# Gate and up products of a gated block: pairs with features in the partitions, regrouped as quads with tokens in the partitions

## The chip, the cores and the metric

One Trainium2 core (of the eight of a chip) runs one layer of an encoder block on 512 tokens of width 1024. The metric is the device time of one execution in microseconds. Names of engines: TensorE (PE; its weight loads are PEld), VectorE (DVE), ScalarE (ACT), GpSimd (POOL), SyncE (SP). [...]

## The reference, cut to what matters

The change lies in the last third, the feed-forward part and the last norm:

```python
h2 = rmsnorm(x, g_ffn[l])
x = x + (jax.nn.silu(h2 @ w_ff_gate[l]) * (h2 @ w_ff_up[l])) @ w_ff_down[l]
return rmsnorm(x, g_final)
```

`h2` is 512 x 1024, `w_ff_gate` and `w_ff_up` are 1024 x 2816 each, `w_ff_down` is 2816 x 1024, all in float32.

## The kernel before

**Products.** Every float32 product is made of three matmuls on split operands: `hi` is the value rounded to the matmul's type by ACT (a CAST, line 203), `lo` is the rest, which DVE makes by a subtraction (line 204); hi·hi, hi·lo and lo·hi are added up in PSUM. Most matrix products of the kernel are then done by a scheme of Strassen's kind: seven products of half-size blocks in place of eight. Each needs a sum of blocks of the weights (`b11`, `t1` to `t4`, `b21`, `b22`; `t1` = b11+b12, `t2` = t1+b22, `t3` = b12+b22, `t4` = t2+b21 in the kernel's signs) and a sum of blocks of the activations (`a11`, `a12`, `a22`, `s1` to `s4`; `XF` holds those of `h2`).

**The feed-forward part before.** The 2816 columns of gate and up are cut into eleven slices of 256. A **pair** (`pair`, with `first_tokens` for two of its products) computes one slice of both. It is feature-major: a 128 x 128 block of the weights is the stationary operand, and the activations of 256 tokens pass over it (`prod`, line 383: 24 matmuls of 256 columns for each of seven products). So the result has features in the partitions, which is what the down product needs, and `gated` (lines 1138 to 1155) makes `silu(gate) * up` and the seven activation forms of the down product from it, slice by slice. The **down** product (`down`, through `strassen` and `prod_tm`, line 427) is token-major: activations stationary, 512 columns of weights moving. It runs after slices 0 to 2, 3 to 6 and 7 to 10 (`FF_PARTS`). The first part's result goes to a buffer `first_part` in device memory, and eight adding DMAs (`add_first`, line 1208) bring it to the sum `ydr` later, behind a one-element POOL instruction `mark` (line 1247) that holds them until slice 3 is gated. The second part adds itself to `ydr`; the last is added to what is read back of it, then normed and stored.

**Weights.** Raw weight tiles of 128 x 1024 come by SP's queue into ten buffers (`load_raws`, line 286). `prefetch_form` adds two raw tiles on DVE where a sum is wanted (line 301) and splits the sum into one of five hi/lo buffers. A product of a pair uses one such tile; a product of a down part uses up to two. `take` prepares two tiles ahead of the product that runs. For the quads in `SUMMED` (two of the eleven pairs, and the product with `w_o`) the four sums are made earlier by adding DMAs of POOL in device memory (lines 272 and 274), and DVE has only the splits.

**Order.** Each engine runs its own list of instructions in a fixed order, decided when the kernel is built from the order of the code and the buffers; an instruction that waits holds up all behind it on its engine, and a DMA that waits holds up its queue.

Of the kernel before, what the change touches and what calls it, by code (L numbers as in the profile page):

```python
# [41 lines left out]
FF_PARTS = ((0, 3), (3, 4), (7, 4))  # L42
# [11 lines left out]
WIDTH = {"w": 512, "x": 256, "a": 512, "o": 512, "f": 256, "d": 512}  # L54
# [4 lines left out]


FIRST_PRODUCTS = ((0, "b11"), (0, "b21"), (1, "b11"), (1, "b21"), (2, "b11"), (2, "b21"))


def beside(q):

    if q < 5:
        return None, ((q + 6) // 2, "b21" if q % 2 else "b11")
    return (q, "b21"), (q + 1, "b11") if q + 1 < NQ else None


def plan():
# [42 lines left out]
    def f(q, *names):  # L114
        for n in names:
            out.append(("q", ("f", q), n, 0, 4))

    for q, name in FIRST_PRODUCTS:
        f(q, name)
    for q0, n in FF_PARTS:  # L120
        for q in range(q0, q0 + n):
            between, behind = beside(q)
            f(q, "t1", "t2")
            if between:
                f(*between)
            f(q, "t3")
            if behind:
                f(*behind)
            f(q, "t4", "b22")
        units = [(name, u) for name in FORMS for u in range(0, n, 2)]  # L130
        if q0 + n == NQ:

            i = units.index(("b21", 2))
            units[i:i + 3] = units[i + 1:i + 3] + units[i:i + 1]
        for name, u in units:
            out.append(("q", ("d", q0), name, u, min(2, n - u)))
    return out
# [9 lines left out]
SUMMED = (("f", 0), ("f", 1), ("o",))  # L147


def parts(quad):  # L150
    return (0, 2) if quad == ("o",) else (0,)
# [20 lines left out]
def block_kernel(ctx: ExitStack, tc: tile.TileContext, xw0, xw, xT, xtok, wpack, wquad, cols, decs, rot, g_ffn, g_final, out):  # L172
# [25 lines left out]
    low_of = [None]  # L198

    def split(src, hi, lo, scale=None, round=None):  # L200
# [4 lines left out]
        else:  # L205
# [3 lines left out]
                op0=ALU.mult, op1=ALU.subtract)  # L209
        return first  # L210
# [51 lines left out]

    steps = {"quads": sums_of(SUMMED[:2]), "heads": sums_of(SUMMED[2:])}

# [25 lines left out]
    def prefetch_form(quad, f, u, nk):  # L290
# [9 lines left out]
        if more:  # L300
            nc.vector.tensor_tensor(out=t, in0=t, in1=raws[quad, more, u][:, 0:n], op=ALU.add)  # L301
        hi, lo = unit()
        split(t, hi[:, 0:n], lo[:, 0:n])
        return [(hi, lo)]

    def prefetch(first=False, loads=None, splits=None):
# [11 lines left out]
        ready.append((x, units))  # L318
        return True
# [708 lines left out]
    def complete(nb, half, last):  # L1028
        yt, ac = y[half][:, nb, :], acs[nb]
        nc.sync.dma_start(ydr[nb * P:(nb + 1) * P, half * 512:(half + 1) * 512], yt)  # L1030
# [83 lines left out]
    gates = {}  # L1114

    q_add, gate_of = FF_PARTS[1][0], [None]

    def act_tiles(names):
        hi, lo = bigtile(F32R), bigtile(F32R)
        for j, n in enumerate(names):  # L1120
            act[n] = tuple(t[:, 2 * j:2 * j + 2, :].rearrange("p a (b c) -> p (a b) c", c=256) for t in (hi, lo))
        return hi.rearrange("p (f a) (b c) -> p f (a b) c", f=2, c=256), \
            lo.rearrange("p (f a) (b c) -> p f (a b) c", f=2, c=256)

    def gated(q, th, g, u):

        q0, _ = part_of[q]
        i = q - q0  # L1130
        if not gates.get(q0):
            t = bigtile(F32R)
            gates[q0] = [act_tiles(("a11", "a12")), act_tiles(("s1", "s3")), act_tiles(("s2", "s4"))]
            act["a22"] = tuple(t[:, 2 * j:2 * j + 2, :].rearrange("p a (b c) -> p (a b) c", c=256)
                               for j in range(2))
# [3 lines left out]
        nc.vector.tensor_tensor(out=s, in0=u, in1=s, op=ALU.mult)  # L1139

        def both(j, t):
            split(t.rearrange("p (s t) -> p s t", s=2), *(x[:, :, i, :] for x in gates[q0][j]))
        E, O = slice(0, 256), slice(256, 512)
        if th == 1:
            split(s[:, O], *(x[:, i, :] for x in act["a22"]))
        else:
            both(0, s)
        gates[q, th] = s
        if (q, 1 - th) not in gates:
            return  # L1150
# [273 lines left out]
```

## Time and profile before

| what | value |
|---|---|
| three timed runs | 1023.89, 1023.9, 1024.5 us; median 1023.9 |
| span of the profiled execution, first to last instruction | 1021.7 us (the page has no time of its own for it) |
| granted TensorE clock, mean | 0.999 |
| feed-forward part in the trace | from about 683.9 us to the end |
| DMA traffic | 202.34 MB, 198 GB/s mean |

The page's first part says how long each engine was busy; the chain of waits follows the execution back from its last instruction to what released each step. Rows with "xN" merge N instructions. An instruction's time runs from its start to its end, and the next one on the same engine may start before that end, so the distance between starts, not the listed duration, says how many fit into a stretch.

### The profile page before, as it was taken

How to read it: one execution, taken by the hardware profiler on the slowest of the kernel's cores; microseconds unless marked ns; L12 is line 12 of the kernel's file. 1: busy time of each engine (PE TensorE's matmuls, PEld its weight loads, DVE VectorE, ACT ScalarE, POOL GpSimd, SP SyncE). 2: the span in 40 equal slices, each digit the busy share in tenths (PEclk: the TensorE clock that was granted, in tenths of full speed). 3: DMA queues.
4: the chain of work that ended last, by engine and by line, in shares of the span. 5: the costliest groups of instructions: out<-in, count | busy, mean ns of one | idle time of the engine just before them, and what ended most of it. 6: DMA issues, size and time to landing. Idle time of an engine off the chain costs nothing.

```text
span 1021.7 us, 14821 instructions
## 1 busy us (share of the span) xinstructions
PE 1013.2 (99%) x5586; PEld 883.2 (86%) x5586; DVE 902.5 (88%) x1161; ACT 548.4 (54%) x744; POOL 151.7 (15%) x238
## 2 busy tenths in 40 slices
PE   9999999999999999999999999999999999999997
PEld 7888888888888998888888888889998999899986
DVE  7878998979798888797989997999898999889996
ACT  7547665553655455343543325586654565556554
POOL 0030221222122003202122100020001410110011
PEclk9999999999999999999999999999999999999999
DMA  9525587695767657839597855484316562663523
GB/s 354 188 81 185 173 296 212 214 310 162 249 196 238 250 203 268 333 130 349 124 331 294 272 200 169 157 264 132 107 42 242 172 154 83 198 153 104 165 69 98
DMA packets 53992, 202.34 MB, mean 198 GB/s; under 512 B 7392, under 2 KB 7520, under 8 KB 49312
## 3 DMA queue, kind: packets, MB, share of 16 engines
q1 hardware_dynamic: 37600, 137.39, 39.0%
q0 software_dynamic: 16032, 63.71, 21.3%
q8 instruction: 44, 0.72, 0.3%
q10 hardware_dynamic: 288, 0.29, 0.1%
q14 instruction: 28, 0.23, 0.1%
HBM read 162.82 MB, written 57.41 MB: 216 GB/s over the span
## 4 chain that ended last, share of the span: by engine, by line
PE 98%; DVE 1%; ACT 0%; issue 0%; POOL 0%; POOLq 0%; ACTq 0%
PE bank L427 39%; PE bank L383 27%; PE bank L342 10%; PE bank L343 10%; PE bank L344 10%; PE bank L477 0%; PE bank L1053 0%; PE bank L998 0%; PE bank L662 0%; DVE raw L301 0%; DVE big L1296 0%; ACT whi L203 0%; DVE wlo L204 0%; POOL fin L1286 0%; POOL ac L1035 0%
## 5 line engine op out<-in xcount | busy, mean ns | idle before, releaser
L203 ACT CAST whi<-raw 128x1024 fp32r<-128x1024 f32 (+2 forms) x299 | 302.8, 1028 | 265.0 <-PE bank L427 67.1
L204 DVE TENSOR_TENSOR wlo<-raw,whi 128x1024 fp32r<-128x1024 f32 (+2 forms) x300 | 352.7, 1192 | 68.0 <-ACT whi L203 67.7
L383 PE MATMUL bank<-xform,whi 128*128 128x256 f32 x1424 | 258.2, 284 | 0.3 <-ACT whi L203 0.3
L383 PEld LDWEIGHTS bank<-xform,whi 128*128 128x128 f32 x1424 | 222.3, 192 | 2.0 <-ACT t L434 0.8
L383 PE MATMUL bank<-xform,wlo 128*128 128x256 f32 x712 | 200.7, 283 | 0.0
L427 PE MATMUL bank<-whi,big 128*128 128x512 f32 x596 | 187.0, 389 | 0.0
L427 PE MATMUL bank<-whi,xform 128*128 128x512 f32 x496 | 157.1, 390 | 0.0
L301 DVE TENSOR_TENSOR raw<-raw 128x1024 f32<-128x1024 f32 (+1 forms) x128 | 152.0, 1203 | 4.2 <-DMA raw<-wquad 3.3
L383 PEld LDWEIGHTS bank<-xform,wlo 128*128 128x128 f32 x712 | 136.4, 192 | 0.0
L427 PEld LDWEIGHTS bank<-whi,big 128*128 128x128 f32 x596 | 111.9, 188 | 23.8 <-ACT t L434 0.4
L427 PE MATMUL bank<-wlo,big 128*128 128x512 f32 x298 | 115.7, 389 | 0.0
L427 PEld LDWEIGHTS bank<-whi,xform 128*128 128x128 f32 x496 | 93.0, 188 | 19.7 <-DVE xform L204 0.6
L427 PE MATMUL bank<-wlo,xform 128*128 128x512 f32 x248 | 96.5, 389 | 0.0
L434 ACT COPY t<-bank 128x512 f32<-128x512 f32 x105 | 61.0, 587 | 56.3 <-PE bank L383 30.1
L342 PE MATMUL bank<-big,whi 128*128 128x512 f32 x220 | 85.7, 390 | 0.0
L344 PE MATMUL bank<-big,wlo 128*128 128x512 f32 x220 | 85.6, 389 | 0.0
L343 PE MATMUL bank<-big,whi 128*128 128x512 f32 x220 | 85.6, 389 | 0.0
L427 PEld LDWEIGHTS bank<-wlo,big 128*128 128x128 f32 x298 | 56.0, 188 | 11.4
L427 PEld LDWEIGHTS bank<-wlo,xform 128*128 128x128 f32 x248 | 46.6, 188 | 9.6
L342 PE MATMUL bank<-whi,big 128*128 128x512 f32 x128 | 49.8, 389 | 0.0
L343 PE MATMUL bank<-wlo,big 128*128 128x512 f32 x128 | 49.8, 389 | 0.0
L344 PE MATMUL bank<-whi,big 128*128 128x512 f32 x128 | 49.8, 389 | 0.0
(203 smaller groups left out, 1385.8 us busy)
## 6 DMA issues: line engine op xcount, KB each, us to landing
raw<-wquad SPq DMA_DIRECT2D x140, 512.0 KB, 4.7
raw<-wpack SPq DMA_DIRECT2D x42, 512.0 KB, 6.3
t_f<-wquad POOLq DMA_DIRECT2D x12, 512.0 KB, 8.0
z<-t POOLq DMA_DIRECT2D x24, 256.0 KB, 4.5
t_o<-wquad POOLq DMA_DIRECT2D x12, 512.0 KB, 6.7
zform<-z POOLq DMA_DIRECT2D x6, 1024.0 KB, 7.8
v<-t POOLq DMA_DIRECT2D x16, 256.0 KB, 5.7
sg<-t POOLq DMA_DIRECT2D x16, 256.0 KB, 4.8
```

Of the source, the lines that this page charges most:

```text
L203: first = (round or nc.scalar.copy)(hi, src)
L204: low_of[0] = nc.vector.tensor_tensor(out=lo, in0=src, in1=hi.bitcast(F32), op=ALU.subtract)
L301: nc.vector.tensor_tensor(out=t, in0=t, in1=raws[quad, more, u][:, 0:n], op=ALU.add)
L342: nc.tensor.matmul(ps, lh, rh, start=first, stop=False)
L343: nc.tensor.matmul(ps, lh, rl, start=False, stop=False)
L344: nc.tensor.matmul(ps, ll, rh, start=False, stop=last)
L383: nc.tensor.matmul(o, l[:, c], r[:, k], start=start and s == 0 and k == 0 and i == 0, stop=stop and k == 3 and i == 2, skip_group_check=True)
L427: nc.tensor.matmul(pss[tt], l, r[:, c], start=start and k == 0 and i == 0, stop=stop and k == n - 1 and i == 2, skip_group_check=True)
L434: nc.scalar.copy(t, ps)
```

## The change

Ten of the eleven slices become five **quads** of two slices each (width 512, kind `g`); the eleventh (`LONE`) stays feature-major.

- A quad is token-major (`first_a`, `first_b`, `rest`, `quad`): 24 matmuls of 512 columns per product, two weight tiles of 1024 columns per product, activations of `h2` stationary.
- Its result has tokens in the partitions. `gated` makes `silu * up` and turns it in 32 x 32 blocks on DVE (line 1213) into `turned`; `scatter` moves the blocks by sixteen SP DMAs (line 1223) into two tiles in which features lie in the partitions; `act_forms_of` (called by `forms_of` in the middle of the next quad) makes the seven forms from there. The tokens come out in another order (32-blocks permuted). It is kept: the rows of `ydr` are written in that order (line 1310, in eight pieces after the first products, where `complete` wrote them as they were done), the lone slice's result is put into the same order (line 1187), and the host reorders the rows of the result.
- The parts are slices 0 to 3, 4 to 7 and 8 to 10, so the down products have 4, 4 and 3 slices where they had 3, 4 and 4.
- Of the weight sums of a quad that is not in `SUMMED`, `t1` and `t2` stay on DVE; `t3` and `t4` are made by POOL DMAs (line 318) that add the second block from device memory onto the raw tile in SBUF, after the last reader of its old content.
- `SUMMED` has quad 0 in place of pairs 0 and 1. The first part's rows go to `first_part` by SP, not POOL.

```diff
-FF_PARTS = ((0, 3), (3, 4), (7, 4))
+FF_PARTS = ((0, 4), (4, 4), (8, 3))
+LONE = NFB // 2 - 1
...
-SUMMED = (("f", 0), ("f", 1), ("o",))
+SUMMED = (("g", 0), ("o",))
+def joined(quad, name):
+    return quad[0] == "g" and quad not in SUMMED and name in ("t3", "t4")
...
-        if more:
+        if more and not joined(quad, f):
             nc.vector.tensor_tensor(out=t, in0=t, in1=raws[quad, more, u][:, 0:n], op=ALU.add)
         hi, lo = unit()
         split(t, hi[:, 0:n], lo[:, 0:n])
+        for g, after, src, add in (("t3", "t1", "b12", "b22"), ("t4", "t2", "b11", "b21")):
+            if f == after and joined(quad, g):
+                late.append((pos[0] + 1, raws[quad, src, u], quarter(quad, add, u), n))
...
+            nc.gpsimd.dma_start(out=t[:, 0:n], in_=src[:, 0:n], accum_op=ALU.add)
...
+    def gated(i, j, g, u):
         s = t512()
         gate_of[0] = s
         nc.scalar.activation(s, g, AF.Silu)
         nc.vector.tensor_tensor(out=s, in0=u, in1=s, op=ALU.mult)
+        for h, t in enumerate(turned[i]):
+            nc.vector.transpose(t[:, :, :, j, :].rearrange("p q i r -> p i q r"),
+                                s.rearrange("p (i q c) -> p i q c", i=4, q=4)[:, :, 2 * h:2 * h + 2, :])
+    def scatter(i):
+        tiles, at = slot(2 * i)
+        x = [area(tiles[k][1], at, 2, k).bitcast(F32) for k in "wv"]
+        for b in range(NB):
+            o = x[b // 2][:, b % 2].rearrange("p q e t -> p (q e t)")
+            for q in range(4):
+                nc.sync.dma_start(o[32 * q:32 * q + 32],
+                                    turned[i][q // 2][32 * b:32 * b + 32, q % 2].rearrange("c i j r -> c (i j r)"))
+    def act_forms_of(q, n, x1, x2):
+        split(flat(x1), flat(hi["a"]), flat(lo["a"]))
+        split(pairs(x2, 1), pairs(hi["z"], 0), pairs(lo["z"], 0))
...
+        for o, a, b, op in ((s1, x[2], x[3], ALU.subtract), (s3, x[0], x[2], ALU.subtract),
+                            (s2, s1, x[0], ALU.subtract), (s4, x[1], s2, ALU.add)):
+            nc.vector.tensor_tensor(out=o, in0=a, in1=b, op=op)
+        for k, e, t in (("v", 1, s1), ("v", 0, s3), ("w", 0, s2), ("w", 1, s4)):
+            split(t, pairs(hi[k], e), pairs(lo[k], e))
+    def first_a(i, *between):
+        a = [bank(), bank()]
+        for u, hook in zip((0, 2), between or (None, None)):
+            prod_tm(4, of(XF[0, 0]), a, True, part=(u,))
+            if hook:
+                hook()
+        heads_of[i] = a, [snap(x) for x in a]
+    def rest(i, last_first=False, middle=True, behind=None):
...
+        prod_tm(4, of(XF[1, 1]), a, False, True)
+        for tt in range(2):
+            gated(i, 2 + tt, a[tt], u3[tt])
+        prod_tm(4, of(XF["s4"]), d, False, True)
+        for tt in range(2):
+            nc.vector.tensor_tensor(out=u2[tt], in0=d[tt], in1=u2[tt], op=ALU.subtract)
+            gated(i, tt, p1[tt], u2[tt])
...
+    rest(0, last_first=True, middle=False)
+    scatter(0)
+    rest(1, behind=lambda: forms_of(0))
+    scatter(1)
+    quad(2, lambda: forms_of(1))
+    down(4, put_first)
+    scatter(2)
+    quad(3, lambda: forms_of(2))
+    mark = small.tile([P, 1], F32, tag="mark", name="mark", bufs=1)
+    add_first(nc.gpsimd.tensor_scalar_add(mark, gate_of[0][:, 0:1], 0.0))
+    scatter(3)
+    quad(4, lambda: forms_of(3))
+    down(4, add_y)
+    scatter(4)
+    lone(lambda: forms_of(4))
...
-    return r.results[0]["y"].reshape(1, S, D)
+    return r.results[0]["y"].reshape(4, 4, 32, D).transpose(1, 0, 2, 3).reshape(1, S, D)
```

What this does to the order on the engines is shown at three places. The first is DVE's list just before the second down product, before the change: the last products of pair 6 are running; `raw` rows are sums of weight tiles for that down product (L301), `wlo` rows splits (L204), L1192 and L1200 the subtractions on the pair's last results, of which L1200 needs the pair's last product.

```order
L301 TENSOR_TENSOR raw_7878<-raw_7878,raw_7943 128x1024
L301 TENSOR_TENSOR raw_7911<-raw_7911,raw_7977 128x1024
L301 TENSOR_TENSOR raw_7943<-raw_7943,raw_8010 128x1024
L204 TENSOR_TENSOR wlo_8101<-raw_7878,whi_8100 128x1024
L1139 TENSOR_TENSOR t512_8040<-t512_7974,t512_8040 128x512
L204 TENSOR_TENSOR wlo_8120<-raw_7911,whi_8119 128x1024
L204 TENSOR_TENSOR big_7332<-t512_8040,big_7332 128x256
L1200 TENSOR_TENSOR t512_7909<-bank_7849,t512_7909 128x512
```

The same place of the changed kernel: DVE's list at the end of quad 4. L1273 are the subtractions that need the quad's last product (one for each half of the tokens), L1209 the gated products, L1213 the turns, L304 the sums and L206 the splits of the down product's `t1` tiles.

```order
L1273 TENSOR_TENSOR t512_7850<-bank_7779,t512_7850 128x512
L1273 TENSOR_TENSOR t512_7852<-bank_7780,t512_7852 128x512
L1209 TENSOR_TENSOR t512_8037<-t512_7850,t512_8037 128x512
L1209 TENSOR_TENSOR t512_8043<-t512_7852,t512_8043 128x512
L1213 STREAM_TRANSPOSE turned_7991<-t512_8037 128x4x2x32
L1213 STREAM_TRANSPOSE turned_7992<-t512_8037 128x4x2x32
L1213 STREAM_TRANSPOSE turned_7991<-t512_8043 128x4x2x32
L1213 STREAM_TRANSPOSE turned_7992<-t512_8043 128x4x2x32
L304 TENSOR_TENSOR raw_7890<-raw_7890,raw_7952 128x1024
L304 TENSOR_TENSOR raw_7908<-raw_7908,raw_7970 128x1024
L304 TENSOR_TENSOR raw_7952<-raw_7952,raw_8000 128x1024
L206 TENSOR_TENSOR wlo_8058<-raw_7890,whi_8057 128x1024
```

Of the three sums the first two are `t1` of the down product (its two tiles), the third belongs to its `t3`. Both tiles of `t1` stood ahead of the subtraction that waits for the last product; now they stand behind it, and behind two gated products and four turns. The end of quad 2 has the same rows.

The second place is the boundary between two quads, quad 1 to quad 2, on DVE and ACT of the changed kernel. DVE's list first, with the names of the place before: here the same tail of the quad is followed by only two sums, both of `t1`, before the `t1` split of the next quad.

```order
L1273 TENSOR_TENSOR t512_6547<-bank_6475,t512_6547 128x512
L1209 TENSOR_TENSOR t512_6739<-t512_6545,t512_6739 128x512
L1209 TENSOR_TENSOR t512_6745<-t512_6547,t512_6745 128x512
L1213 STREAM_TRANSPOSE turned_6693<-t512_6739 128x4x2x32
L1213 STREAM_TRANSPOSE turned_6694<-t512_6739 128x4x2x32
L1213 STREAM_TRANSPOSE turned_6693<-t512_6745 128x4x2x32
L1213 STREAM_TRANSPOSE turned_6694<-t512_6745 128x4x2x32
L304 TENSOR_TENSOR raw_6585<-raw_6585,raw_6654 128x1024
L304 TENSOR_TENSOR raw_6603<-raw_6603,raw_6672 128x1024
L206 TENSOR_TENSOR wlo_6772<-raw_6585,whi_6771 128x1024
```

ACT's list at the same boundary; L449 copies a bank of the next quad's first product to SBUF (a snapshot), L205 are casts of weight tiles, of which `whi_6771` belongs to the `t1` tile above.

```order
L449 COPY t512_6807<-bank_6766 128x512
L205 CAST whi_6771<-raw_6585 128x1024
L449 COPY t512_6809<-bank_6767 128x512
L205 CAST whi_6790<-raw_6603 128x1024
L205 CAST whi_6814<-raw_6585 128x1024
```

The cast of `t1`'s first tile, `whi_6771`, stands behind the copy of the first bank of the next quad's first product. At the boundary of two pairs before, no turns stood there, and the next tile was split ahead of the last subtraction. The boundary from quad 3 to quad 4 has the same rows.

The third place is POOL's queue around `mark`. Before, the eight adding DMAs of `first_part` are followed by nothing until the second down product.

```order
L1211 DMA first_part_6056<-t512_7033 128x512
L1211 DMA first_part_6056<-t512_7035 128x512
L1247 TENSOR_SCALAR mark_7389<-t512_7374 128x1
L1208 DMA ydr_5321<-first_part_6056 128x512 x8
L1208 DMA ydr_5321<-t512_8135 128x512
```

Now the adding DMAs for `t3` and `t4` of quads 3 and 4 (L318) stand ahead of `mark` and behind the eight.

```order
L318 DMA raw_7282<-wquad 128x1024
L318 DMA raw_7300<-wquad 128x1024
L318 DMA raw_7236<-wquad 128x1024
L318 DMA raw_7255<-wquad 128x1024
L1321 TENSOR_SCALAR mark_7708<-t512_7703 128x1
L1282 DMA ydr_5321<-first_part_6048 128x512 x8
L318 DMA raw_7612<-wquad 128x1024
L318 DMA raw_7630<-wquad 128x1024
L318 DMA raw_7543<-wquad 128x1024
L318 DMA raw_7561<-wquad 128x1024
```

The tiles 7612 and 7630 are `t3` of quad 4, 7543 and 7561 its `t4`: their sums are issued only when POOL has done `mark` and the eight DMAs.

More of the change, by code (lines that the diff above doesn't have):

```diff
@@ L1113, in block_kernel @@
     act = {}
[L1114 to L1125, printed above, removed]
[L1129 to L1135 removed]
+    slots = {}
```

217 lines of the change are left out of this document (119 added, 98 removed).

## The prediction

> **What bounds the kernel now.** I read the page's busy times first, then its chain of waits, then what TensorE waited for, and last the feed-forward part stage by stage.
>
> ```profile
> PE 1013.2 (99%) x5586; PEld 883.2 (86%) x5586; DVE 902.5 (88%) x1161; ACT 548.4 (54%) x744; POOL 151.7 (15%) x238
> ...
> PE 98%; DVE 1%; ACT 0%; issue 0%; POOL 0%; POOLq 0%; ACTq 0%
> ```
>
> The first line is busy time by engine, the second the chain's shares: PE is busy 99% of the span and is 98% of the chain. So a cheaper matmul shows in the time, and so does every stall of PE; work of another engine counts only where PE runs out.
>
> ```profile
> PE bank L1053 <- DVE t L1039: 0.5, 1, 0.5
> PE bank L383 <- ACT whi L203: 0.3, 1, 0.3
> ```
>
> These are PE's waits (total, times, longest): two short ones near or in the feed-forward part, from 683.9 us on. Its room beside PE is in the table of windows (width, then busy time of PE, PEld, DVE, ACT, POOL, clock, DMA share, GB/s):
>
> ```profile
> 824.00:861.40 37.40, 37.40 (x314) 37.40 (x313) 36.18 (x45) 22.12 (x31) 0.00 (x0) 1.00 0.44 131
> 861.40:899.50 38.10, 38.10 (x171) 31.54 (x169) 34.86 (x39) 20.16 (x25) 5.26 (x6) 1.00 0.57 149
> ...
> sum 321.20, PE 320.86 PEld 301.92 DVE 296.47 ACT 186.15 POOL 31.02; mean PE 35.65 PEld 33.55 DVE 32.94 ACT 20.68 POOL 3.45
> ```
>
> The granted clock is 1.00 in all. DVE is busy 296.5 of 321.2 us (0.92), so it has little to give where an order turns against it.
>
> **The change part by part.**
>
> *Matmuls.* Ten pairs of 168 matmuls of 256 columns (1680) go; five quads of 168 matmuls of 512 columns (840) come. Both forms run now, and the chain shows stretches of each (start, us, what):
>
> ```profile
> 787.53 73.91 PE bank L383 x612
> 861.44 38.11 PE bank L427 x168
> ```
>
> 73.91/612 = 0.1208 us; 38.11/168 = 0.2269 us, in a down product whose form is that of a quad. 1680 x 0.1208 = 202.9 against 840 x 0.2269 = 190.6: **-12.3 us**. The window from 824.0, all of the narrow form, has 314 in 37.40 us: 0.1191, which gives 9.5, the lower bound. I take the longer stretch. The down products have the same eleven slices in all, and the lone slice stays as it was: nothing.
>
> [...]
>
> *DVE work.*
>
> ```profile
> L301 DVE TENSOR_TENSOR raw<-raw 128x1024 f32<-128x1024 f32 x124 | 149.4, 1220 | 1.6 <-DMA raw<-wquad 0.8
> ...
> 443.03 7.13 DVE L218 STREAM_TRANSPOSE big<-big 32x512 f32<-32x512 f32 x10
> 871.21 4.62 DVE L204 TENSOR_TENSOR wlo<-raw,whi 128x1024 fp32r<-128x1024 f32 x4
> 1002.80 1.28 DVE L1273 TENSOR_TENSOR big<-bank,big 128x512 f32<-128x512 f32 x2
> ```
>
> Adding DMAs take over `t3` and `t4` of four quads, two tiles each: 16 sums of 1.22 = -19.5 us. Each quad turns its result in eight transposes. No row has their shape. A row of 32x512 costs 0.71; half its columns are 0.36 if time goes with columns, 0.71 if it doesn't. I take 0.43, nearer to the first because the other DVE rows go with columns (starts 1.14 us apart at 1024, 4.62 = 3 x 1.14 + 1.2, and 0.60 at 512, 1.28 = 0.60 + 0.68): 40 x 0.43 = +17.2. Wider gated products and forms take some 4 us less. DVE's total hardly moves, and PE hides it; what counts is the order.
>
> *The end of a quad.* This is the unknown wait, seen nowhere in before. Let E be the end of the quad's last product. At 1010.21 a subtraction on DVE starts 0.02 us after its product's end, so take E as its start:
>
> ```profile
> 1010.19 0.02 issue
> 1010.21 0.69 DVE big L1273
> ...
> L203 ACT CAST whi<-raw 128x1024 fp32r<-128x1024 f32 x287 | 296.8, 1049 | 255.8 <-PE bank L427 61.0 <-DVE raw L301 47.0 <-PE bank L344 41.2
> ```
>
> One subtraction is done ahead of E (it belongs to the first half of the tokens), the second by E+0.8. Two gated products to 2.0, four transposes at 0.43 to 3.7, two `t1` sums to 4.9 and 6.0. ACT casts the first tile behind a copy of the next product's first bank, from 4.9 to 6.0. The split's `lo` follows on DVE to 7.3. PE has one product meanwhile, 24 x 0.2269 = 5.44. Then two matmuls need only `hi` and the rest need `lo`: it waits 5.44 to 6.0, works 0.45, waits to 7.3: **1.4 us**. This happens after quads 1 and 3: **+2.8 us**. With transposes of 0.36 and no queueing of the copy it is 0.9 each; with 0.71 it is 2.5.
>
> Before a down product a third sum stands in between: `lo` at 8.4, a wait of 2.5. The split may come later still by the adding DMAs of the same quad. `t4`'s second is issued after the `t2` split, some 14.1 us after the quad's start, and the hi/lo buffer that its split wants is free at 20.4, so it has 6.3 us to land. The nearest rows:
>
> ```profile
> t_f<-wquad POOLq DMA_DIRECT2D x12, 512.0 KB, 8.0
> ...
> big<-ydr POOLq DMA_DIRECT2D x4, 256.0 KB, 4.5
> ...
> DMA to landing us min/median/max: 3.6/5.6/9.4
> ```
>
> (KB each and median us to landing; the last row is that of all transfers of the `t_f` tiles.) An adding DMA into SBUF of half the size took 4.5, one of the size into device memory 8.0. I take 6.5, between them, which puts 0.4 on it: 2.9 after quads 2 and 4, **+5.8 us**, between 2.0 and 5 each without and with late landings.
>
> *The lone slice and the tail.* At the lone slice's end silu and products of the same kind stand ahead of the last split; I allow 1.0 (0 to 1.4), for the 0.3 that PE waits now: **+0.7**. The last down part has three slices, so the last product has 18 matmuls for 24 behind the first half's result:
>
> ```profile
> 1014.48 0.72 ACT L1298 ACTIVATE big<-big,fin 128x512 f32<-128x512 f32 x1 [0.24 <-POOL fin L1286]
> 1015.65 0.60 ACT L1337 ACTIVATE t<-bank 128x512 f32<-128x512 f32 x1 [0.45 <-PE bank L427]
> ```
>
> PE ends 1.36 us (6 x 0.2269) earlier against the norm's work, but ACT stands only 0.45 behind it there; the rest, **+0.9**, is lost.
>
> *Hidden.* `scatter` is 16 DMAs on SP:
>
> ```profile
> 962.93 0.38 SPq L1258 DMA_DIRECT2D big<-ydr  x1
> ...
> y<-big SPq DMA_DIRECT2D x7, 256.0 KB, 2.1
> ```
>
> At 0.38 an issue, 6.1 us and a landing of about 2.1: 8.2 after the last turn. The forms are wanted in the middle of the next quad, over 13 us later; PE's 38 us quad hides it, and weights queued behind it on SP are for products a quad later. If 5 us longer, nothing shows. The first part's rows on SP rather than POOL, and the eight `ydr` rows written later, lie behind whole products too. `SUMMED` moves as many bytes as before, eight tiles.
>
> *Sum:* -12.3 + 2.8 + 5.8 + 0.7 + 0.9 = -2.1. From the span of 1021.7 that is 1019.6; the median stands 2.2 above the span (1023.9): **1021.8 us**.
>
> **The rivals.**
>
> *The waits don't come (R1).* The two transposes of the second token half could overlap what I have in line, or the buffers carry PE over. For it: before, PE never ran dry at a boundary with a split like this one behind its last product:
>
> ```profile
> 862.32 0.68 DVE L1200 TENSOR_TENSOR t<-bank,t 128x512 f32<-128x512 f32 x1
> ...
> 866.26 1.22 DVE L204 TENSOR_TENSOR wlo<-raw,whi 128x1024 fp32r<-128x1024 f32 x1
> ```
>
> That `lo` is done 5.2 us after the subtraction's start, and PE didn't wait. Against it: mine comes at 7.3 or 8.4. Time: -12.3 + 0.9, so 1012.5.
>
> *Slower: POOL is late (R2).* The adding DMAs of quad 4 stand behind `mark` and eight others:
>
> ```profile
> 805.94 7.34 POOL L1247 TENSOR_SCALAR mark<-t 128x1 f32<-128x1 f32 x1 [17.56 <-DVE t L1139]
> 813.24 6.82 POOL L1208 DMA_DIRECT2D ydr<-first_part  x8
> ```
>
> If `mark`, free at 2.0 us after quad 3, takes 7.3 again, the eight are out at 16.2, `t3`'s first tile lands at 16.2 + 0.9 (its issue) + 6.5 = 23.6 and has its `lo` 2.3 later, at 25.9. PE wants it at 1.4 + 4 x 5.44 + 0.45 = 23.6: a wait of 2.3. `t4`'s second is issued at 16.2 + 3 x 0.9 = 18.9, lands at 25.4, 2.7 after its buffer (20.4 + 2.3): 2.5 more before the down product. Time 1021.8 + 4.8 = **1026.6**, slower. It decides once `mark` and the eight take over some 12 us together. Against it: why `mark` took so long.
>
> ```profile
> 805.76 1.22 DVE L204 TENSOR_TENSOR wlo<-raw,whi 128x1024 fp32r<-128x1024 f32 x1
> ...
> 813.20 0.69 DVE L1192 TENSOR_TENSOR t<-bank,t 128x512 f32<-128x512 f32 x1
> ...
> L1277 POOL TENSOR_SCALAR fin<-fin x4: 183/189/942, 1004.3 to 1007.7; 128x1 f32<-128x1 f32 x4
> ```
>
> The same operation on one column took 0.19 elsewhere. `mark` starts just after a DVE operation on two SBUF tiles, and ends as the first one that reads PSUM begins; between them DVE ran without a gap. Now it becomes free ahead of four transposes, with one input each, so it should be short. [...]
>
> *Adding DMAs land slowly (R3).* At 9.4 us, the slowest of the `t_f` rows, `t4`'s second lands 3.1 after its buffer and not 0.2: +2.9 at each of the two down boundaries, 1027.6. For it: scatters, weights and eight adding DMAs now share the engines. Against it: the windows' DMA share is 0.44 to 0.57.
>
> *The change doesn't do what it says (R4):* the wide matmul is no cheaper here. The down product's row has the same form, so it would need quads with other pauses. [...]
>
> **How the numbers follow.** My forecast 0.44, R1 0.20, R2 0.12, R3 0.20, R4 0.04. The forecast's own range is 1018 to 1026, by the ends of the waits: all at their lower ends 3.5 below, one of the two kinds at its upper end up to 4.2 above. The range reaches down to R1 and up past R3: 1012.5 to 1028.5. A measurement tells 0.2% (2 us) from no change, and 1021.8 lies on that bound: of the forecast's 0.44, 0.20 is faster, 0.19 same, 0.05 slower. R1 is faster; R2, R3 and R4 are slower but for 0.05 of R3. Faster 0.40, same 0.24, slower 0.36.
>
> **What the profile after would show.** A stretch of 168 wide matmuls of a quad at 38.1 us bears out the first term; PE's list of waits should hold two of about 1.4 us and two of about 2.9 on `lo` tiles of `t1`. No such waits: R1. Waits on `hi` or `lo` of `t3` tiles in quad 4, and `mark` over 5 us: R2. Adding DMAs with a median above 8 us, and later splits at the down boundaries: R3. It would be wrong altogether if PE waited on `scatter` or on weights behind it on SP.

## The result, and the profile after

The changed kernel takes 1041.43 us (median of four; 1040.98 to 1042.17) against 1023.89 us before: ratio 1.0176, 95% interval 1.0161 to 1.019. It is slower by 17.5 us. The profiled execution took 1040.98 us with a span of 1039.2 us, 17.5 above the 1021.7 of before, so the two traces can be set against each other.

The first two lines of the page that stood ahead of the prediction, now of the changed kernel (busy time by engine, then the chain's shares):

```profile
PE 1010.1 (97%) x4746; PEld 842.5 (81%) x4746; DVE 895.4 (86%) x1163; ACT 547.6 (53%) x736; POOL 154.2 (15%) x246
...
PE 82%; DVE 7%; issue 5%; DMA 2%; SPq 1%; POOL 1%; ACT 1%; POOLq 0%; DVEq 0%; ACTq 0%
```

PE has 840 matmuls fewer and is busy only 3.1 us less, in a span that is 17.5 us longer. The chain leaves PE for 18% of its length; before it was 2%. What PE waited for (total, times, longest):

```profile
PE bank L442 <- ACT t L449: 9.1, 2, 7.3
PE bank L442 <- DVE wlo L206: 4.2, 4, 1.6
PE bank L442 <- ACT whi L205: 4.0, 4, 1.3
```

The second and third row are the waits at the ends of quads, 8.2 us in all, where the prediction had 8.6. The first row was not in the forecast's sum. In the timeline of PE the wait of 7.3 us is at 908 us, at the product of quad 4 that uses `t3` (start, duration, xcount, and in brackets the idle time before):

```profile
907.62 0.39 PE L442 MATMUL bank<-whi,xform 128*128 128x512 f32 x1
915.31 0.80 PE L442 MATMUL bank<-whi,xform 128*128 128x512 f32 x1 [7.30 <-ACT t L449]
915.90 0.63 PE L442 MATMUL bank<-wlo,xform 128*128 128x512 f32 x1
916.33 1.05 PE L442 MATMUL bank<-whi,xform 128*128 128x512 f32 x2
917.18 0.63 PE L442 MATMUL bank<-wlo,xform 128*128 128x512 f32 x1
917.61 1.02 PE L442 MATMUL bank<-whi,xform 128*128 128x512 f32 x2
918.46 0.40 PE L442 MATMUL bank<-wlo,xform 128*128 128x512 f32 x1
918.70 0.63 PE L442 MATMUL bank<-whi,xform 128*128 128x512 f32 x2
```

The row's releaser, a copy on ACT, is the last link of a chain that begins at the `t3` tiles:

```profile
911.08 1.04 ACT L205 CAST whi<-raw 128x1024 fp32r<-128x1024 f32 x1 [11.56 <-DMA raw<-wquad]
913.73 1.04 ACT L205 CAST whi<-raw 128x1024 fp32r<-128x1024 f32 x1 [1.60 <-DMA raw<-wquad]
914.68 1.06 ACT L449 COPY t<-bank 128x512 f32<-128x512 f32 x2
```

ACT stands idle until each `t3` tile has landed, casts it, and only then makes the two copies, which stand behind the casts in its list. The product adds to the bank that they copy, so PE goes on when the first copy ends, at 915.3. The wait of 1.8 us at 924 us has the same form: its copies start at 923.73, behind the casts of `t4`, of which the last could start only at 919.41, and four more casts.

Two things are to be seen. The `t3` tiles came late. And behind the wait PE is slow: from 915.90 on starts are 0.43 us apart (915.90, 916.33, then two in 0.85), until 918.5; from there two take 0.46 again. These matmuls are busy time, so no list of waits shows them. The table of windows does, in the column behind POOL's, the granted clock:

```profile
812.00:850.00 38.00, 38.00 (x162) 31.26 (x161) 32.94 (x32) 20.06 (x23) 2.40 (x3) 0.96 0.53 152
...
898.00:936.00 38.00, 28.87 (x113) 22.89 (x112) 22.33 (x29) 17.41 (x24) 1.98 (x3) 0.87 0.78 207
936.00:950.00 14.00, 11.32 (x43) 8.59 (x42) 14.00 (x19) 4.71 (x6) 0.00 (x0) 0.88 0.00 1
```

Before, it was 1.00 in every window of this part. Summed over the timeline, starts that are further apart than 0.227 us cost 1.7 us behind the wait of 810 us, 1.6 behind each of 908, 922 and 944 us: 6.5 us.

Why the `t3` tiles were late stands in POOL's timeline and in the list of transfers issued from 884 to 925 us (KB each, median us to landing):

```profile
887.11 0.22 POOL L1321 TENSOR_SCALAR mark<-t 128x1 f32<-128x1 f32 x1 [35.03 <-DVE t L1209]
887.62 6.79 POOL L1282 DMA_DIRECT2D ydr<-first_part  x8 [0.28 <-issue]
894.77 0.91 POOL L318 DMA_DIRECT2D raw<-wquad  x1 [0.36 <-DMA ydr<-first_part]
```

```profile
ydr<-first_part POOLq DMA_DIRECT2D x8, 256.0 KB, 10.4
raw<-wquad POOLq DMA_DIRECT2D x4, 512.0 KB, 16.7
```

`mark` took 0.22 us, the eight adding transfers were out at 894.4, and the first of `t3` was issued at 894.77, about where the prediction's times put it with a short `mark`. It then took some 16 us to land, where 6.5 were forecast.

The end is late too. PE's last matmul ends at 1029.8, and the span ends 9.4 us later; before, these were 1015.6 and 6.1 us.

So the 17.5 us are: matmuls -11 (measured in late_ahead, below), waits at the ends of quads +8.2, waits in quad 4 +9.1, half pace +6.5, the end +3.3. That is 16.1; the other 1.4 are spread over the stretches and are not traced further.

### The profile page after: what moved, and what is told of

Its sections match the earlier page's. It is cut to its first block, busy times and chain, and to the rows that moved or that the text cites. A ratio compares the mean times of both kernels' runs of the same rounds, so it can differ in the third digit from the quotient of the medians.

```text
span 1039.2 us, 13337 instructions
## 1 busy us (share of the span) xinstructions
PE 1010.1 (97%) x4746; PEld 842.5 (81%) x4746; DVE 895.4 (86%) x1163; ACT 547.6 (53%) x736; POOL 154.2 (15%) x246
## 4 chain that ended last, share of the span: by engine, by line
PE 82%; DVE 7%; issue 5%; DMA 2%; SPq 1%; POOL 1%; ACT 1%; POOLq 0%; DVEq 0%; ACTq 0%
PE bank L442 44%; PE bank L357 10%; PE bank L359 10%; PE bank L358 10%; PE bank L398 8%; DMA raw<-wquad 2%; DVE wlo L206 2%; SPq L1223 1%; DVE big L206 1%; DVE raw L304 1%; DVE turned L1213 1%; DVE t L1173 1%; DVE t L1209 1%; POOL ydr L1282 0%; PE bank L492 0%
## 5 line engine op out<-in xcount | busy, mean ns | idle before, releaser
L205 ACT CAST whi<-raw 128x1024 fp32r<-128x1024 f32 (+2 forms) x299 | 302.5, 1028 | 263.2 <-PE bank L442 78.8
L206 DVE TENSOR_TENSOR wlo<-raw,whi 128x1024 fp32r<-128x1024 f32 (+2 forms) x300 | 351.5, 1190 | 95.0 <-ACT whi L205 94.5
L442 PE MATMUL bank<-whi,xform 128*128 128x512 f32 x1056 | 333.7, 393 | 10.8 <-ACT t L449 9.1
L442 PEld LDWEIGHTS bank<-whi,xform 128*128 128x128 f32 x1056 | 199.4, 189 | 54.6 <-ACT t L449 10.0
L442 PE MATMUL bank<-wlo,xform 128*128 128x512 f32 x528 | 207.0, 392 | 1.1 <-DVE wlo L206 1.1
L304 DVE TENSOR_TENSOR raw<-raw 128x1024 f32<-128x1024 f32 x112 | 131.6, 1197 | 0.8
L442 PE MATMUL bank<-wlo,big 128*128 128x512 f32 x298 | 117.8, 395 | 3.3 <-DVE wlo L206 3.2
L442 PEld LDWEIGHTS bank<-wlo,xform 128*128 128x128 f32 x528 | 99.9, 189 | 22.4 <-DVE wlo L206 1.9
L449 ACT COPY t<-bank 128x512 f32<-128x512 f32 x105 | 61.0, 586 | 80.9 <-PE bank L442 63.6
L398 PE MATMUL bank<-xform,whi 128*128 128x256 f32 x304 | 55.3, 283 | 0.2 <-ACT t L449 0.2
L358 PE MATMUL bank<-wlo,big 128*128 128x512 f32 x128 | 49.8, 389 | 0.0
L359 PEld LDWEIGHTS bank<-big,wlo 128*128 128x128 f32 x220 | 41.3, 188 | 8.7
L358 PEld LDWEIGHTS bank<-big,whi 128*128 128x128 f32 x220 | 41.3, 188 | 8.6
L357 PEld LDWEIGHTS bank<-big,whi 128*128 128x128 f32 x220 | 41.3, 188 | 8.5
```

The lines of the kernel that those rows point to most:

```text
L205: first = (round or nc.scalar.copy)(hi, src)
L206: low_of[0] = nc.vector.tensor_tensor(out=lo, in0=src, in1=hi.bitcast(F32), op=ALU.subtract)
L357: nc.tensor.matmul(ps, lh, rh, start=first, stop=False)
L358: nc.tensor.matmul(ps, lh, rl, start=False, stop=False)
L359: nc.tensor.matmul(ps, ll, rh, start=False, stop=last)
L398: nc.tensor.matmul(o, l[:, c], r[:, k], start=start and s == 0 and k == 0 and i == 0, stop=stop and k == 3 and i == 2, skip_group_check=True)
```

## Experiments

All ratios are to the kernel before, run beside them on the same chip.

| label | what is different | us, median | ratio, 95% interval |
|---|---|---|---|
| changed kernel | | 1041.43 | 1.0176 (1.0161 to 1.019) |
| late_add | eight adding transfers after quad 4 | 1029.67 | 1.0059 (1.0044 to 1.0074) |
| ahead3 | three tiles ahead | 1038.56 | 1.0144 (1.0129 to 1.0159) |
| late_ahead | both | 1022.9 | 0.9995 (0.9985 to 1.0005) |
| fill | extra matmuls in the waits | 1038.51 | 1.0149 (1.0132 to 1.0166) |
| held4 | late_ahead, four ahead, turns held | 1025.01 | 1.0013 (1.0004 to 1.0023) |
| nojoin | no adding transfers onto raw tiles | 1025.65 | 1.0026 (1.0012 to 1.004) |
| nojoin_late | nojoin and late_add | 1025.72 | 1.0031 (1.0015 to 1.0048) |
| tail_join | late_add, last `t3`, `t4` by transfers | 1027.38 | 1.0036 (1.0023 to 1.0049) |
| held4_tail | held4 and that | 1025.93 | 1.0021 (1.0011 to 1.0031) |
| tail_fill | late_add, extra matmuls at the end | 1029.36 | 1.0056 (1.0041 to 1.0071) |
| mid_fill | late_ahead, extra matmuls in the waits | 1022.89 | 0.9992 (0.9984 to 1.0001) |
| combined | late_ahead, mid_fill, tail_join | 1022.01 | 0.9976 (0.9965 to 0.9988) |

**The late transfers: late_add, nojoin, nojoin_late.**

```diff
-    mark = small.tile([P, 1], F32, tag="mark", name="mark", bufs=1)
-    add_first(nc.gpsimd.tensor_scalar_add(mark, gate_of[0][:, 0:1], 0.0))
     scatter(3)
     quad(4, lambda: forms_of(3))
+    mark = small.tile([P, 1], F32, tag="mark", name="mark", bufs=1)
+    add_first(nc.gpsimd.tensor_scalar_add(mark, gate_of[0][:, 0:1], 0.0))
     down(4, add_y)
```

> Edit: the eight adding transfers of the first part's rows (and the one-element operation that holds them) are issued after quad 4 instead of before it. Theory A (these eight crowd the four adding transfers of quad 4's t3 and t4, which landed 16 to 18 us after issue): the four land in about 7.5 us, the median of all such transfers, PE's waits of 7.3 and 1.8 us in quad 4 go, and with them about 4 us of matmuls at half pace after them: 1041.4 - 13 = 1028 us, with the four waits at the ends of the quads still there. Rival B (the scatter and the weight loads crowd them): they still take over 12 us, time 1036 to 1041. Rival C (only their place in POOL's queue counts, they are issued 10 us late): they are issued before 885 us of the trace and the time is 1028 too, but transfers in other quads would not be slow.

1029.67 us, 11.8 less. PE has no wait in quad 4 but the one at its start. The transfers issued from 884 to 925 us, first those of late_add:

```profile
raw<-wquad POOLq DMA_DIRECT2D x4, 512.0 KB, 7.6
big<-turned SPq DMA_DIRECT2D x16, 64.0 KB, 5.7
```

The four land in 7.6 us, with the sixteen of the scatter still beside them, so the scatter (B) is not what held them. Theory A has the time and the waits right. Its word "crowd" is another matter, and so is C, by which the four were only issued late. The landing times of the eight (shortest, median, longest), in the changed kernel and in the kernel before, say more:

```profile
DMA to landing us min/median/max: 4.6/10.4/14.7
DMA to landing us min/median/max: 4.8/8.4/10.3
```

The eight are issued mostly half a microsecond apart, but they land one behind another, some 2 us apart, the last at 907.2. The four follow in the order of their issue: 911.0, 913.6, 916.1 and 919.3. In the packets of POOL's queue those of the eight run from 889 to 907 us, and those of the four from 904 to 919. In late_add, without the eight, the four move from 893 to 907, and in nojoin, below, the eight without the four from 886 to 902. So each kind takes about as long to move with the other as without it. The four were not slowed; they stood in POOL's queue behind what was issued and not yet moved of the eight's 2 MB.

nojoin takes the other side away:

```diff
 def joined(quad, name):
-    return quad[0] == "g" and quad not in SUMMED and name in ("t3", "t4")
+    return False
```

> Edit, from the changed kernel: all four sums of a quad on DVE again, no adding transfer onto a raw tile; everything else as changed, the eight adding transfers of the first part's rows before quad 4 too. Theory A (the adding transfers of quad 4's t3 and t4 are what PE waited 9.1 us for, as they were crowded by the eight): that wait goes, with 4 us of half pace, but DVE gets 4 sums of 1.2 us more in each of four quads, which is 19.5 us of work in some 190 us where DVE was busy 0.9: waits at the ends of quads grow by 1 to 2 us each: 1041.4 - 13 + 6 = 1034 us. Rival (DVE has room for them in the middle of the quads): 1028. Rival (DVE is full): above 1041.

1025.65 us: 15.8 less than the changed kernel, 4.0 less than late_add. The eight transfers, now with only scatter and weight loads beside them, land about as in the changed kernel:

```profile
ydr<-first_part POOLq DMA_DIRECT2D x8, 256.0 KB, 9.8
big<-turned SPq DMA_DIRECT2D x16, 64.0 KB, 5.9
```

and nothing waits for them. The nearest expectation was the rival by which DVE has room for the 16 sums (1028); the growth of the waits that theory A had added for DVE, 6 us, didn't come: waits at the ends of quads sum to 7.7 us, not 8.2. So this part of the change is worth less than nothing here: DVE does the sums in time that PE doesn't miss, and the transfers that replace them hold PE up where they stand behind others. Of the 4.5 us between the profiles of late_add and nojoin, 1.8 are shorter waits at the ends of quads (9.5 in late_add) and some 1.7 one stretch of half pace less.

> Edit: nojoin and late_add together, so neither adding transfers onto raw tiles nor the eight adding transfers in quad 4. Theory A (the eight do harm only because the four of quad 4's t3 and t4 stand among them): no further gain, 1024 to 1026.5 us. Rival (the eight delay weights or scatter by themselves): 2 us or more below nojoin's 1025.65, under 1023.6.

1025.72 us, no change. The eight do no harm by themselves; it takes both kinds at once.

**The waits at the ends of quads: ahead3, late_ahead, held4.**

```diff
-        while sum(len(u) for _, u in ready) < AHEAD and prefetch():
+        while sum(len(u) for _, u in ready) < ahead[0] and prefetch():
...
+    ahead[0] = 3
     rest(0, last_first=True, middle=False)
```

> Edit: from quad 0 on, three weight tiles are prepared ahead of the product that runs, not two, so that the first t1 tile of the next quad or down product is split ahead of the last gated products and turns. Theory A (the waits at the ends of quads are the t1 split standing behind the turns, and each is followed by about 3 us of matmuls at half pace): the waits of 0.9, 2.9, 1.9 and 2.7 us fall to under 0.5 each, PE's granted clock in the stretches behind them goes to 1.00, 1041.4 - 8 - 6 = 1027 us; the waits in quad 4 stay. Rival B (the wait only moves, to t1's second tile or to the down products' sums): time above 1035.

1038.56 us, 2.9 less and not 14: a miss. The wait moved, as the rival said. DVE's timeline of the changed kernel at the end of quad 2, where PE's last product ended at 802.5:

```profile
803.28 1.27 DVE L1273 TENSOR_TENSOR t<-bank,t 128x512 f32<-128x512 f32 x2
804.48 1.28 DVE L1209 TENSOR_TENSOR t<-t,t 128x512 f32<-128x512 f32 x2
805.67 1.41 DVE L1213 STREAM_TRANSPOSE turned<-t 128x256 f32<-128x256 f32 x4
807.01 3.45 DVE L304 TENSOR_TENSOR raw<-raw 128x1024 f32<-128x1024 f32 x3
810.38 2.35 DVE L206 TENSOR_TENSOR wlo<-raw,whi 128x1024 fp32r<-128x1024 f32 x2
```

and of late_ahead, which has this edit too, at the same place:

```profile
803.54 1.28 DVE L1274 TENSOR_TENSOR t<-bank,t 128x512 f32<-128x512 f32 x2
804.74 1.23 DVE L206 TENSOR_TENSOR wlo<-raw,whi 128x1024 fp32r<-128x1024 f32 x1
805.89 1.29 DVE L1210 TENSOR_TENSOR t<-t,t 128x512 f32<-128x512 f32 x2
807.09 1.42 DVE L1214 STREAM_TRANSPOSE turned<-t 128x256 f32<-128x256 f32 x4
808.43 3.45 DVE L304 TENSOR_TENSOR raw<-raw 128x1024 f32<-128x1024 f32 x3
811.80 2.35 DVE L206 TENSOR_TENSOR wlo<-raw,whi 128x1024 fp32r<-128x1024 f32 x2
```

In the first, both `t1` tiles are split last, behind turns and three sums: the chain that the prediction wrote down, with turns of 0.33 us from start to start, where 0.43 was taken. In the second one tile is split at 804.74, ahead of them, and the other waits as long as before, so PE stops 2.7 us in the middle of `t1` rather than 2.9 ahead of it. DVE has no gap in either piece.

> Both edits: the eight adding transfers after quad 4, and three weight tiles prepared ahead. If the two causes are separate and the matmuls' saving of 12.3 us is real, the two gains add up: 1041.4 - 13 - 14 = 1014 us. If they share a cause (a busy DVE, or shared transfer engines), the sum is short by 5 us or more: 1020 or above.

1022.9 us, the speed of the kernel before, 6.8 below late_add where ahead3 had gained 2.9. The 1014 of separate causes was missed by 9, and 1020 or above came true; but the two edits together gain 18.5 us, more than the 11.8 and 2.9 that they gain singly. What failed is the 14 us that ahead3 was thought to be worth.

> Edit, on top of late_ahead: four weight tiles are prepared ahead from quad 0 on, and the turns of a quad's last two results stand behind the last split made so far, so both t1 tiles are split ahead of the turns. Theory A (the 2.7 and 2.4 us that PE still waits at the two down products of late_ahead are t1's second tile behind the turns and three sums): PE waits there for under 0.6 us, matmuls keep full pace, a down product takes under 39.5 us where it took 43.3 and 42.8: 1022.9 - 8 = 1015 us. Rival B (DVE is simply full from the middle of the last quad to the middle of the down product, so a wait returns at t2 or t3): the stretches stay above 41.5 us, 1019 us or more.

```diff
+        low = low_of[0]
         for tt in range(2):
             nc.vector.tensor_tensor(out=u2[tt], in0=d[tt], in1=u2[tt], op=ALU.subtract)
-            gated(i, tt, p1[tt], u2[tt])
+            gated(i, tt, p1[tt], u2[tt], (low,))
```

(The turns in `gated` are then issued behind `low`, the last split so far; four tiles ahead.) The down products fall to 41.0 and 40.1 us, from 43.3 and 42.8, but waits of 1.4 us, each in two pieces, return inside both and inside quads 2 and 4, and one of 1.2 at the last down product: 1025.01 us, 2.1 above late_ahead. The stretches lie between the two theories (39.5 and 41.5); the time and the waits that return are rival B's. DVE has no gap over 0.3 us from 789 to 833 us, from the second half of quad 2 into the down product, so an order can only choose which tile is late.

**The half pace: fill, mid_fill.**

```diff
+        if fill:
+            for _ in range(fill[1]):
+                nc.tensor.matmul(fill[0], xh, wh[:, c], start=True, stop=True, skip_group_check=True)
```

> Edit: after the b11 product of quads 2 and 4 six, and of the first two down products twelve extra matmuls (1.4 and 2.7 us at full pace) are put into a PSUM bank that the next product starts afresh, where PE stood still. The outputs are the same. Theory A (a wait is followed by half-pace matmuls because the array stood idle): the waits are as long as before but filled, so the stretch of a down product falls from 43.1 and 42.8 to about 41 us, and two quads lose 1 us less each: 1041.4 - 6 = 1035.5 us, granted clock 1.00 there. Rival (half pace has another cause, such as operands or banks): 1041 or, where the extra matmuls overshoot, 1042.

1038.51 us, 2.9 less, half of what was expected. With the extra matmuls the two down products take 41.82 and 41.84 us instead of 43.12 and 42.83, the longest wait left in them is 0.5 us, and the clock stays at 1.00; that is 2.3 of it. The quads gained nothing: they lost as much to the extra matmuls as to the wait. At 0.85 and 1.85 us of wait, in two pieces, PE had not lost its pace there.

> Edit, on top of late_ahead: between the two tiles of t1 in the first two down products PE gets eight extra matmuls (1.8 us at full pace) into a bank that is started afresh later, where it stood still for 1.8 us. Nothing else moves. Theory A (after a wait of some 1.5 us the matmuls run at half pace for about 3 us): the wait is as long but the half pace goes, so the down products fall from 43.3 and 42.8 to about 41 us, granted clock 1.00 there, and the time from 1022.9 to 1019 us, faster than before the change by over 0.2%. Rival (what is lost behind the wait is DVE's late next tiles, not PE's pace): the stretches stay above 42.5, 1022 to 1023.5 us.

In the profiles the down products fell from 43.26 and 42.82 to 41.29 and 41.83 us with a clock of 1.00, as theory A has it. The time didn't follow: 1022.89 against 1022.9, where the rival had it. A likely reason, not shown, as each kernel has one profile: the profiled execution of late_ahead was its slowest (1025.39 us, mean clock 0.994); eight of its ten have 0.996 to 0.998, so they may have lost their pace less often to begin with. Pace isn't all: the profile of mid_fill (1025.03 us, its slowest) has no stretch of half pace, but a wait of 1.7 us at the start of quad 4 that is 0.4 in late_ahead. How much an execution loses to the pace shows most clearly in nojoin, whose executions fall into groups by it:

```
mean clock 0.997: 1023.46  1023.53  1023.24
mean clock 0.996 or 0.995: 1025.26  1025.13  1026.05
mean clock 0.992: 1028.29  1028.5  1028.19  1028.41
```

These are steps of 2 to 3 us in one program. Its profile has both cases, two waits of the same length at two down products (the wait is the bracketed one; what follows it is the pace):

```profile
811.39 0.50 PE L442 MATMUL bank<-wlo,big 128*128 128x512 f32 x1 [1.42 <-DVE wlo L206]
811.73 0.62 PE L442 MATMUL bank<-whi,big 128*128 128x512 f32 x2
812.19 0.40 PE L442 MATMUL bank<-wlo,big 128*128 128x512 f32 x1
...
930.23 0.80 PE L442 MATMUL bank<-wlo,big 128*128 128x512 f32 x1 [1.41 <-DVE wlo L206]
930.83 1.06 PE L442 MATMUL bank<-whi,big 128*128 128x512 f32 x2
931.68 0.63 PE L442 MATMUL bank<-wlo,big 128*128 128x512 f32 x1
```

After 1.42 us the next two start 0.23 apart; after 1.41 us 0.43. The length of a wait doesn't decide it: behind one of 1.87 us in late_add, at 891.4 us, starts are 0.23 apart too. The table of windows of nojoin, cut into stretches of 3.41 us from the time at which its clock falls behind the second wait, 930.21 (width, PE's busy time, ..., and the clock third from the end):

```profile
807.34:810.75 3.41, 2.32 (x9) 1.26 (x8) 3.41 (x4) 2.96 (x4) 0.00 (x0) 1.00 0.00 0
810.75:814.16 3.41, 2.77 (x12) 2.30 (x13) 3.41 (x4) 0.52 (x1) 0.00 (x0) 1.00 0.00 0
926.80:930.21 3.41, 1.70 (x7) 0.77 (x5) 3.41 (x4) 2.67 (x4) 0.00 (x0) 1.00 0.00 0
930.21:933.63 3.42, 3.40 (x8) 2.75 (x9) 3.42 (x4) 1.06 (x2) 0.00 (x0) 0.50 0.00 0
```

Ahead of each of the two waits PE stood still once more, for 0.32 us. The first pair is parted at 810.75, and PE stands still for 1.09 us of one stretch and 0.64 of the next. The second pair lies in one stretch, in which PE stands still for 1.71 us, half of it; the stretch behind has half the clock. The traces of the changed kernel and of the kernel before can be cut in the same way. In the changed kernel's the clock changes, up to PE's last matmul, at 812.66, 816.07, 911.64, 918.47, 925.30, 928.71, 945.78 and 949.19 us, whole multiples of 3.41 us apart. Four of its stretches at full clock have half clock behind them, and in these PE stands still for 1.67, 3.41, 1.83 and 2.44 us; in no other at full clock, from 20 us of the trace on, is it more than 1.32. In the trace of the kernel before no stretch up to PE's last matmul has more than 1.36 us, and the clock is 1.00 throughout. So a wait that costs more than its length in one execution and not in the next is, as far as these three traces tell, a matter of how the standstill is spread over such stretches. In nojoin_late the waits are those of nojoin to 0.01 us, the clock is 1.00 in every window from 765 to 965 us, where nojoin has 0.96 from 921 to 965, and the span is 1021.7 us against 1023.5. A stretch at half pace cost up to 1.7 us in the changed kernel; with the extra matmuls of fill and mid_fill the first two down products had none.

**The end: tail_join, held4_tail, tail_fill.**

> Edit, on top of late_add: t3 and t4 of the last down product too are made by adding transfers, so DVE has four sums (2 x 1.14 and 2 x 0.60 us) less before the last norm. Theory A (the end comes 9.7 us behind PE's last matmul, not 6.1 as before the change, because the last part's three slices leave DVE's list late against PE): 9.7 falls to about 7.5, 1029.7 - 2.5 = 1027 us. Rival (the last product's 18 matmuls leave the norm's own chain too little time, whatever stands before it): 9.7 stays, 1029.5 us; if the four transfers are late, slower.

1027.38 us, as expected in size, but not where: the span ends 9.3 us behind PE's last matmul, against 9.7. These four sums don't make the distance: in late_add they lie ahead of 1007.0 us, and DVE then waits 0.7 us for PE. Of the 1.8 us between the two profiles 0.8 lie in the last down product and behind it; the rest lies in stretches that the edit doesn't touch, so the gain isn't shown to be the edit's.

> Edit, on top of late_add: six extra matmuls in each of the last two products of the last down part, so that each has 24 as before the change, in a bank of their own. Theory A (DVE's fixed work for the last norm sets the end, and the shorter last part gives nothing): PE ends 2.7 us later, the end comes 7.0 to 7.5 us behind it and not 9.7, the time stays at 1029.7 +- 0.7 us. Rival (PE sets the end): 1032.4 us.

```diff
+    spare = bank()
-    prod_tm(n, forms["a22"], a, False, True, ev_a)
-    prod_tm(n, forms["s4"], d, False, True, ev_d)
+    prod_tm(n, forms["a22"], a, False, True, ev_a, fill=spare)
+    prod_tm(n, forms["s4"], d, False, True, ev_d, fill=spare)
```

(Three extra matmuls behind each half.) 1029.36 us against 1029.67, and the end comes 7.4 us behind PE's: nine matmuls, 2.0 us, ahead of PE's last useful one cost nothing, so PE's last two products don't set the end. In late_add DVE has no gap from 1007.7 to 1019.3, with the last splits, the sums of the result and the norm's products one behind the other; the last part's 28.6 us of PE leave its fixed work less time than the 38.1 us of before.

> held4 and tail_join together: 1015 - 2.5 = 1012.5 us if both theories hold. At 1015 only the boundary theory holds; at 1019 or above neither.

1025.93 us: neither theory holds. A wait of 1.4 us comes in the last down product that held4 and tail_join don't have, and what tail_join gained on late_add is not gained on held4.

**A kernel faster than both: combined.**

> Edit: late_add, three tiles ahead in the quads (two again from the lone slice on), the eight extra matmuls of mid_fill and the adding transfers of tail_join. Theory (the loss is the sum of parts that hardly touch each other: quad 4's late adding transfers, the waits at the ends of quads, the half pace behind them, and DVE's work at the end): mid_fill's 1022.9 less the 2.3 us that tail_join gained on late_add, 1020.6 us, faster than before the change by 0.3%. Rival (what is gained at one place is lost in the next, since DVE is nearly full from the second quad on): 1022 to 1024 us.

1022.01 us, ratio 0.9976 (0.9965 to 0.9988): a quarter of a per cent below the kernel before. The 1020.6 of the theory was missed by 1.4; the time lies at the lower end of the rival's range. In its profile PE waits 2.8 us in the feed-forward part, where it waits 17.5 in the changed kernel, and never falls to half pace. Of the 11 us or so that the matmuls save, these waits take 2.8, the end 3.1 and the sixteen extra matmuls 3.6; that leaves about the 1.5 us by which the two spans differ.

## Why the prediction was wrong

- **Matmuls.** -12.3 us was about -11: in late_ahead quads 3 and 4 take 77.2 us with one wait of 0.4, 38.4 each, where two pairs took 2 x 168 x 0.1208 = 40.6. That is 2.2 a quad, 11 in all. R4 is out.
- **Ends of quads.** 1.4 each between quads: 0.85 and 1.85. 2.9 each ahead of a down product: 2.84 and 2.69. The mechanism, its place and the sum (8.2 for 8.6) were right. The size is in part luck: at the end of quad 2 a split stands ahead of the subtractions, so the first gated product starts 1.8 us behind PE's last matmul and not 0.8, while the four turns took 0.4 less and no landing was late, for which 0.4 was added. R1 is out. The lone slice's 1.0 was 0.2.
- **The step that failed first: "I take 6.5" for the landing of an adding transfer**, and with it a wait in quad 4 that the sum puts at nothing. In quad 4 the landing took 16 to 18 us, and PE waited 9.1 us. The range, 4.5 to 9.4, came from other stretches, where no eight others stood ahead in POOL's queue. R2 had the place, POOL's queue behind `mark` and the eight. It was thought to fall with a short `mark`, and `mark` was short (0.22 us); what had held it for 7.34 us before, no run isolates. But the eight behind `mark` were counted for the 6.8 us of their issue, and not for the 17.5 us in which they moved. The profile of the kernel before could have told: the same eight landed 4.8 to 10.3 us after issue, the last 15.4 us after the first was issued. R3 had the sign, landings over 8 us, but not the cause. Shown by late_add and nojoin together, 11.8 and 15.8 us, and by the order of landing.
- **The step that was missing: a wait costs its own length.** No part of the sum, no rival and no bound had the pace behind a wait. The granted clock of 1.00 was quoted as a fact about this part, but it was read in a profile in which PE hardly stopped (0.5 us at most in this part), and behind four stops of the changed kernel it was 0.50. That is 6.5 us in the profile.
- **The end.** 0.9 was 3.3 us: ACT's margin of 0.45 was read, DVE's work ahead of it wasn't. With tail_join, which takes four sums from DVE, 3.2 are left. What remains is DVE's work from 1007.7 us on, in late_add's times, and the chain of waits of the changed kernel ends in the same work.
- **Hidden.** `scatter` took 11 to 20 us of SP and not 6.1, as each of the sixteen issues takes 0.5 us and more. The chain of waits runs through it once, yet PE has no wait that ends with it, and in late_add the four adding transfers were quick beside it. No run isolates it.

The range ended at 1028.5 because the rivals were priced one at a time, R2 with the wrong size. The measured time has R2's place, the eight transfers' moving time and the pace behind the waits.

## What to carry to other kernels

Where the bounding engine is to be made faster, price what a stop of it costs beyond its length: in the changed kernel the matmuls behind four stops ran at half pace, with a clock of 0.50, and that took 6.5 us beyond the waits themselves. Two short waits close together, 1.09 and 1.59 us at 944 us, cost as much in this way as one of 7.30, 1.6 us each. A transfer's landing time from a quiet stretch is no price for a stretch in which others stand ahead of it in its queue; count the time in which those move, not only their issues (17.5 us and 6.8 for the eight here). Taking work from an engine that is nearly full but not the bound can lose, if what replaces it has a deadline: without the adding transfers onto raw tiles the kernel was 15.8 us faster.

## What had not been expected of the hardware

- Half pace came behind some waits and not behind others of the same length: in nojoin a wait of 1.41 us brought it and one of 1.42 didn't, nor did two of 1.62 and 0.94 with two matmuls between them, which lie in two of the stretches above. What differs in the traces is the standstill in one stretch of 3.41 us: 1.71 us in nojoin and 1.67 or more in the changed kernel ahead of half clock, 1.32 at most elsewhere in the changed kernel. It cost 1.6 to 1.7 us each time in the changed kernel. It cost 3.0 once, in ahead3, where starts were 0.43 apart from 913.4 to 918.9 us, behind a wait of 6.65. Executions of one program that differ by 5 us differ in their mean clock too, 0.997 and 0.992, about what three such stretches would make (an estimate, at 1.7 us each).
- In the changed kernel the adding transfers on POOL's queue moved in the order of their issue, packets of the eight from 889 to 907 us and of the four from 904 to 919, and the four took no longer behind the eight than alone in late_add (893 to 907). The weight loads on SP in the same stretch didn't wait for them: they landed 5.8 us after issue (median) with the eight there, and 6.7 in late_add, without.
